# Turning cached attention keys on VectorE, sharing the runs of two sample groups, and 512-column matmuls for the memory keys and values

## The chip, the cores and the metric

The kernel runs on one core of a Trainium2 chip. The metric is the device time of one execution in microseconds, as the median over several executions. The trace is of one execution that the hardware profiler recorded.

## The reference

One inference step of a two-layer streaming encoder is computed for two groups of inputs at once: a prompt of 512 new frames, and 8 running streams (the samples) with 16 new frames each behind 256 cached ones. The part that matters here is the mixer of the first layer (forgetting attention, 16 heads of 64), and the keys and values of the memory for both layers:

```
def fox_mixer(h, q_pos, past, w_in, b_f, w_out):
    ...
    k_all = jnp.concatenate([past[0], k], axis=1)
    v_all = jnp.concatenate([past[1], v], axis=1)
    ...
    s = jnp.einsum('bqhd,bkhd->bhqk', qb, k_all).astype(jnp.float32) * FOX_SCALE
    s = s + jnp.moveaxis(cqb, 1, 2)[..., None] - ck
    p = masked_softmax(s, mask).astype(v_all.dtype)
    return jnp.einsum('bhqk,bkhd->bqhd', p, v_all)

def memory_kv(mem, g_mem, w_x_kv):
    m_l = rms_normalize(mem)[None] * g_mem[:, None, None, :]
    kv = jnp.einsum('lbnd,lde->lbne', m_l, w_x_kv)
    k, v = jnp.split(kv, 2, axis=-1)
```

For the samples `past[0]` is the cached keys, `cache_fox_k`, of shape (1, 8, 256, 16, 64). `mem_prompt` has 256 rows of 1024, and `w_x_kv` is (2, 1024, 2048). All is float32.

## The kernel before

The first phase, `fox_phase`, goes through the 16 heads in eight pairs. For each pair `pr` three lists of steps are merged by `merge`: `prompt_list` (attention of the prompt, 9 steps), `sample_list` (attention of the samples, 14 steps) and a fill of projections for the next pairs: `k_list`, `v_list`, `q_list` and `out_list`. A step stands at the place (i + 0.5) / length of its list, and the merged order is the order in which instructions are emitted. The tile framework's planner then makes each engine's queue out of that order by priority, modelled durations and free buffers; at run time each queue is in order. The pools name how many buffers a tile has (`bufs`); an instruction that needs a buffer waits until the last reader of its former content is done.

A big matrix product is made of three passes of float32r matmuls (`PASSES`: high by high, high by low, low by high). `load_w` brings a weight unit of 128 x 1024 values into `raw` (2 buffers), ScalarE casts it to `whi` (L150), and VectorE subtracts to get `wlo` (L151), with 3 buffers each. All of the kernel's DMAs are issued on SyncE's queue (SP).

`sample_list` handles the eight streams as two groups of four (`bq` = 0 and 1), one after the other. For each group `load` fetches the cached keys (`kr`, L654, one buffer, tokens on the partitions, 1,024 pieces of 512 bytes) and values (`vr`, L656), `keys` turns 8 blocks of 128 x 128 by TensorE in two visits of 4 (L664), and the results are copied out of PSUM into `KT` by VectorE (L668) for the first half and ScalarE (L670) for the second. `scores` does the matmuls of L685 and the softmax, and builds a block-diagonal copy of the new frames' weights on VectorE (L694). `trans` turns the weights (L701), `values` multiplies by the values (L710), and `turn` turns the result back (L717) and gates it (L722). VectorE also copies the new keys into `KT` (L658).

`mem_list` makes the memory's keys and values of one layer. Its first group of steps normalises the 256 memory rows and turns them into `mT`; eight more groups each handle 256 output columns: a load of two weight units, two products of 24 matmuls with 256 columns (one for each 128 memory rows, each in its own PSUM bank and in two parts), a copy to `mrow` by ScalarE (L373), and a store. Of the 18 groups of both layers, the first 7 are fill of pair 6, the next 9 of pair 7, and the last 2 come after all pairs.

## Time and profile before

| | |
|---|---|
| median of 3 runs | 2115.81 us (2113.45 to 2122.21) |
| the profiled execution: time | 2118.55 us |
| the profiled execution: span of the core | 2116.8 us |
| mean granted TensorE clock | 0.998 |
| TensorE matmul busy | 2066.9 us, 98% of the span |
| TensorE weight loads busy | 1857.4 us, 88% |
| VectorE, ScalarE, GpSimd busy | 1393.1, 900.0 and 176.0 us (66%, 43%, 8%) |

The span is the time from the first to the last instruction of the core; 1.75 us of the execution's time lie outside it. Busy times are unions of the instructions' spans. A matmul's span begins before the one ahead of it has ended, so one matmul's duration is longer than the step from one matmul to the next. In rows of the trace PE is TensorE's matmuls, PEld its weight loads, DVE VectorE, ACT ScalarE, POOL GpSimd, and SP SyncE with a q for its queue of DMA issues.

### The profile page before, as it was taken

The page shows a single profiled execution, that of the slowest core. Times are in us where ns is not written, and L with a number is a line of the kernel's source. Part 1 is how long each engine was busy: PE and PEld are TensorE (multiplying, and loading weights), DVE is VectorE, ACT ScalarE, POOL GpSimd, SP SyncE. Part 2 cuts the span into 40 slices and gives each one's busy share as a digit, 9 for nine tenths or more (in the row PEclk, how much of TensorE's full clock was granted, in tenths as well). Part 3 has the DMA queues.
Part 4 walks back from the last instruction along what each step waited for, and adds up shares of the span by engine and source line. Part 5 has one row for each costly group of instructions (what it writes and reads, how often), then busy time and mean ns, then how long its engine had stood idle before and what let it go on. Part 6 is the DMA issues. An engine that isn't in the chain of part 4 may idle for free. (4 is left out here: it accounts for less than half of the span.)

```text
span 2116.8 us, 35888 instructions
## 1 busy us (share of the span) xinstructions
PE 2066.9 (98%) x14189; PEld 1857.4 (88%) x14189; DVE 1393.1 (66%) x2695; ACT 900.0 (43%) x1793; POOL 176.0 (8%) x362
## 2 busy tenths in 40 slices
PE   7999999999999999999999999999999999999998
PEld 7988888889987899999998978887887799999997
DVE  4454555564646796686686567767546896686686
ACT  4444444454443453343344455554443453343342
POOL 1121212120100000000001301100100000000000
PEclk9999999999999999999999999999999999999999
DMA  7443434477555322232221331112554322232221
GB/s 225 130 137 107 139 112 130 147 230 224 166 165 172 100 72 83 85 91 79 81 80 50 92 95 39 53 44 77 164 167 157 100 74 84 83 92 79 80 81 60
DMA packets 279279, 234.33 MB, mean 111 GB/s; under 512 B 15668, under 2 KB 255924, under 8 KB 279112
## 3 DMA queue, kind: packets, MB, share of 16 engines
q1 hardware_dynamic: 279112, 232.05, 36.0%
q8 instruction: 112, 1.84, 0.4%
q14 instruction: 55, 0.45, 0.1%
HBM read 214.80 MB, written 17.21 MB: 110 GB/s over the span
## 5 line engine op out<-in xcount | busy, mean ns | idle before, releaser
L204 PE MATMUL mm<-hT,whi 128*128 128x320 f32 x1744 | 291.5, 313 | 3.8 <-ACT hT L222 3.8
L204 PEld LDWEIGHTS mm<-hT,whi 128*128 128x128 f32 x1744 | 260.9, 188 | 9.8 <-ACT hT L222 5.2
L151 DVE TENSOR_TENSOR wlo<-raw,whi 128x1024 fp32r<-128x1024 f32 (+4 forms) x145 | 170.1, 1176 | 144.2 <-ACT whi L150 84.8
L318 DVE TENSOR_TENSOR X<-mm,X 128x512 f32<-128x512 f32 x270 | 182.8, 686 | 123.1 <-PE mm L204 121.8
L150 ACT CAST whi<-raw 128x1024 fp32r<-128x1024 f32 (+4 forms) x145 | 144.6, 1002 | 150.8 <-PE mm L204 103.4
L204 PE MATMUL mm<-whi,oT 128*128 128x512 f32 x544 | 182.9, 410 | 1.9 <-DVE X L318 1.1
L1103 ACT CAST whi<-tw 128x512 fp32r<-128x512 f32 (+1 forms) x120 | 91.9, 765 | 213.7 <-PE mm L204 127.5
L204 PE MATMUL mm<-whi,aT 128*128 128x512 f32 x560 | 173.0, 390 | 0.3 <-ACT aT L1068 0.3
L204 PE MATMUL mm<-hT,wlo 128*128 128x320 f32 x872 | 156.8, 312 | 0.0
L204 PEld LDWEIGHTS mm<-hT,wlo 128*128 128x128 f32 x872 | 133.4, 188 | 3.2 <-issue 3.1
L204 PE MATMUL mm<-whi,hT 128*128 128x256 f32 (+2 forms) x800 | 127.5, 298 | 2.4 <-ACT whi L150 1.5
L204 PE MATMUL mm<-s,whi 128*128 128x320 f32 x768 | 128.2, 309 | 0.0
L204 PEld LDWEIGHTS mm<-whi,aT 128*128 128x128 f32 x560 | 104.4, 188 | 22.6 <-ACT aT L1068 1.2
L232 POOL TENSOR_SCALAR rstd<-ss 128x1 f32<-128x1 f32 x49 | 17.2, 352 | 1266.0 <-ACT hn L230 1261.5
L204 PEld LDWEIGHTS mm<-whi,oT 128*128 128x128 f32 x544 | 96.6, 189 | 23.2 <-issue 3.7
L204 PEld LDWEIGHTS mm<-whi,hT 128*128 128x128 f32 x800 | 110.0, 193 | 7.7 <-issue 3.9
L204 PEld LDWEIGHTS mm<-s,whi 128*128 128x128 f32 x768 | 116.6, 188 | 0.0
L1104 DVE TENSOR_TENSOR wlo<-tw,whi 128x512 fp32r<-128x512 f32 (+1 forms) x120 | 103.4, 862 | 18.9 <-ACT whi L1103 18.4
L204 PE MATMUL mm<-wlo,oT 128*128 128x512 f32 x272 | 109.1, 401 | 0.0
L204 PE MATMUL mm<-wlo,aT 128*128 128x512 f32 x280 | 108.8, 389 | 0.0
L1103 ACT CAST whi<-raw 128x1024 fp32r<-128x1024 f32 x44 | 46.3, 1052 | 131.7 <-PE mm L204 72.3
L204 PE MATMUL ps_s<-whi,aT 128*128 128x512 f32 x320 | 98.6, 389 | 0.0
(340 smaller groups left out, 4280.5 us busy)
## 6 DMA issues: line engine op xcount, KB each, us to landing
rawg<-w_ffn_gu SPq DMA_DIRECT2D x80, 512.0 KB
raw<-w_ffn_down SPq DMA_DIRECT2D x44, 512.0 KB
raw<-w_x_kv SPq DMA_DIRECT2D x32, 512.0 KB
kr<-cache_mem_k SPq DMA_DIRECT2D x64, 256.0 KB
vr<-cache_mem_v SPq DMA_DIRECT2D x32, 512.0 KB
raw<-w_fox_in SPq DMA_DIRECT2D x30, 512.0 KB
kr<-cache_fox_k SPq DMA_DIRECT2D x16, 512.0 KB
vr<-cache_fox_v SPq DMA_DIRECT2D x16, 512.0 KB
```

The costliest lines, as they stand in the source:

```text
L150: A.copy(hi[:, 0:m], raw[:, 0:m])
L151: V.tensor_tensor(lo[:, 0:m], raw[:, 0:m], hi[:, 0:m].bitcast(F32), ALU.subtract)
L204: T.matmul(st["ps"][:, 0:n], lhsT=l, rhs=r, start=(j == 0), stop=(j == m - 1))
L232: G.tensor_scalar(r, ss, EPS, None, ALU.add)
L318: V.tensor_tensor(xs, ps, xs, ALU.add)
L1103: A.copy(hi[:, o:o + m], src)
L1104: V.tensor_tensor(lo[:, o:o + m], src, hi[:, o:o + m].bitcast(F32), ALU.subtract)
```

## The change

Four things change in `fox_phase` and `mem_list`.

- The cached keys arrive in another order. Token 32m + j of a stream lies on partition j of a block of 32 partitions, and four DMAs for each group, one for each 32 channels of the pair's 128, fill the four blocks of partitions. `V.transpose` then turns blocks of 32 x 32 straight from `kr` into `KT`, 512 columns an instruction, two for each group. There are no TensorE transposes of keys, and no copies out of PSUM for them. `kr` has 2 buffers and `KT` 3.
- The copy of the new keys into `KT` and the block-diagonal product move from VectorE to GpSimd.
- The two groups of streams go through one list of 13 steps: both loads first, then four `keys` steps, two `bias` steps, one `scores` step with the matmuls of both groups in two PSUM banks, two `trans` steps, one `values` step into one bank, and one `turn` step with two transposes and two gating products twice as wide.
- `mem_list` has four groups for 512 output columns each in place of eight for 256. A group holds two PSUM banks open, one for each 128 memory rows, and goes through the 1024 input rows in four parts: a weight unit of 256 rows by 512 columns, then 6 matmuls of 512 columns into each bank. Each part's unit is loaded one part ahead. Of the 10 groups now, 4 are in pair 6, 5 in pair 7 and 1 after the pairs.

```diff
@@ -354,23 +354,36 @@
             to_T(h, d["mT"], t * P, KD)
 
         groups = [[gains, lambda: norm(0), lambda: norm(1)]]
-        for h in range(4):
+        for c0 in range(0, D, 512):
             for i in range(2):
-                c0 = i * D + h * XD
                 u = {}
 
-                def load(u=u, c0=c0):
-                    u["w"] = load_w([(0, XD, w_kv[:, c0:c0 + XD])])
-                    u["row"] = pool().tile([P, 2, XD], F32, tag="mrow", name="mrow", bufs=2)
-
-                def store(u=u, i=i, h=h):
-                    S.dma_start(outs[i][:, :, h * XD:(h + 1) * XD], u["row"])
-                    S.dma_start(kvd[l][i].rearrange("(t p) n -> p t n", p=P)[:, :, h * XD:(h + 1) * XD], u["row"])
-
-                L = [load]
-                for t in range(2):
-                    L += gemm(lambda u=u, t=t: as_ops(d["mT"], slice(t * P, (t + 1) * P), u["w"], slice(0, XD), KD),
-                              XD, lambda ps, u=u, t=t: A.copy(u["row"][:, t, :], ps[:, 0:XD]), parts=2)
+                def load(m, u=u, c=i * D + c0):
+
+                    if m == 0:
+                        u["row"] = pool().tile([P, 2, 512], F32, tag="mrow", name="mrow", bufs=2)
+                    u[m] = load_w([(0, 512, w_kv[:, c:c + 512])], k0=2 * m, kt=2, per=2)
+
+                def part(m, u=u):
+                    for t in range(2):
+                        if m == 0:
+                            u["ps", t] = psum_mm()
+                        ops = [(d["mT"][ai][:, 2 * m + k, t * P:(t + 1) * P], u[m].get(wi, k))
+                               for wi, ai in PASSES for k in range(2)]
+                        for n, (l, r) in enumerate(ops):
+                            T.matmul(u["ps", t], lhsT=l, rhs=r, start=(m == 0 and n == 0), stop=(m == 3 and n == 5))
+                        if m == 3:
+                            A.copy(u["row"][:, t, :], u["ps", t])
+
+                def store(u=u, i=i, c0=c0):
+                    S.dma_start(outs[i][:, :, c0:c0 + 512], u["row"])
+                    S.dma_start(kvd[l][i].rearrange("(t p) n -> p t n", p=P)[:, :, c0:c0 + 512], u["row"])
+
+                L = [lambda load=load: load(0)]
+                for m in range(4):
+                    if m < 3:
+                        L.append(lambda load=load, m=m: load(m + 1))
+                    L.append(lambda part=part, m=m: part(m))
                 groups.append(L + [store])
         return groups
 
@@ -378,7 +391,7 @@
     def fox_phase():
         w_in = I["w_fox_in"][0]
         w_out = I["w_fox_out"][0]
-        ck = I["cache_fox_k"][0].rearrange("b (tt t) h d -> t (b tt) (h d)", t=P)
+        ck = I["cache_fox_k"][0].rearrange("b (m j) h d -> j (b m) (h d)", j=32)
         cv = I["cache_fox_v"][0].rearrange("b (tt t) h d -> t (b tt) (h d)", t=P)
         ko = O["fox_k_p"][0, 0].rearrange("(t p) h d -> p t (h d)", p=P)
         vo = O["fox_v_p"][0, 0].rearrange("(t p) h d -> p t (h d)", p=P)
...
@@ -650,28 +663,23 @@
                 d = {}
 
                 def load(bq):
-                    d["kr"] = fp.tile([P, 8, P], F32, tag="kr", name="kr", bufs=1)
-                    S.dma_start(d["kr"], ck[:, 8 * bq:8 * bq + 8, pr * P:(pr + 1) * P])
-                    d["vr"] = fp.tile([P, 8, P], F32, tag="vr", name="vr", bufs=2)
-                    S.dma_start(d["vr"], cv[:, 8 * bq:8 * bq + 8, pr * P:(pr + 1) * P])
-                    d["KT"] = fp.tile([P, 4, KS], F32, tag="KT", name="KT", bufs=2)
-                    V.tensor_copy(d["KT"][:, :, PAST:KS],
+
+                    kr = d["kr", bq] = fp.tile([P, 32, 32], F32, tag="kr", name="kr", bufs=2)
+                    for i in range(4):
+                        c0 = pr * P + 32 * i
+                        S.dma_start(kr[32 * i:32 * i + 32], ck[:, 32 * bq:32 * bq + 32, c0:c0 + 32])
+                    d["vr", bq] = fp.tile([P, 8, P], F32, tag="vr", name="vr", bufs=2)
+                    S.dma_start(d["vr", bq], cv[:, 8 * bq:8 * bq + 8, pr * P:(pr + 1) * P])
+                    d["KT", bq] = fp.tile([P, 4, KS], F32, tag="KT", name="KT", bufs=3)
+                    G.tensor_copy(d["KT", bq][:, :, PAST:KS],
                                   ks[pr][1][:, bq * 64:(bq + 1) * 64].rearrange("p (b t) -> p b t", t=TS))
 
-                def keys(b2):
-                    pt = psum_t()
-                    for i in range(4):
-                        T.transpose(out=pt[:, i * P:(i + 1) * P], in_=d["kr"][:, 4 * b2 + i, :], identity=ident)
-                    src = pt[:, :].rearrange("p (b t) -> p b t", t=PAST)
-                    dst = d["KT"][:, 2 * b2:2 * b2 + 2, 0:PAST]
-                    if b2 == 0:
-                        V.tensor_copy(dst, src)
-                    else:
-                        A.copy(dst, src)
-
-                def scores(bq):
-                    Q = qs_[pr][1]
-                    pw = d["pw"] = pw_tile()
+                def keys(bq, b2):
+                    V.transpose(d["KT", bq][:, 2 * b2:2 * b2 + 2, 0:PAST],
+                                d["kr", bq][:, 16 * b2:16 * b2 + 16, :].rearrange("p (b m) i -> p b (m i)", b=2))
+
+                def bias(bq):
+                    pw = d["pw", bq] = pw_tile()
                     r0 = 16 * pr + 8 * bq
                     S.dma_start(pw[:, 0:KS], csd[r0:r0 + 8].unsqueeze(1).broadcast_to([8, TS, KS]))
                     jk = small.tile([P, TS], F32, tag="jk", name="jk")
@@ -680,53 +688,60 @@
                                            op0=ALU.mult, op1=ALU.add, accum_out=cqs)
                     G.tensor_scalar(pw[:, 0:KS], pw[:, 0:KS], -1.0, cqs, ALU.mult, ALU.add)
                     G.tensor_tensor(pw[:, PAST:KS], pw[:, PAST:KS], cm16, ALU.add)
-                    sp = psum_s()
-                    for b in range(4):
-                        T.matmul(sp[32 * b:32 * b + 32, 0:KS], lhsT=Q[:, 4 * bq + b, :], rhs=d["KT"][:, b, :],
-                                 start=True, stop=True, tile_position=(0, 32 * b))
-                    nm = small.tile([P, 1], F32, tag="nm", name="nm")
-                    V.tensor_tensor_reduce(out=pw[:, 0:KS], in0=sp[:, 0:KS], in1=pw[:, 0:KS], scale=-1.0,
-                                           scalar=3.0e38, op0=ALU.add, op1=ALU.min, accum_out=nm)
-                    ss = small.tile([P, 1], F32, tag="ssum", name="ssum")
-                    A.activation(pw[:, 0:KS], pw[:, 0:KS], AF.Exp, scale=-1.0, bias=nm, accum_out=ss)
-                    softmax_tail(pw, ss, KS)
-                    bm = cst[:, C_BM + P * bq:C_BM + P * (bq + 1)]
-                    V.tensor_tensor(pw[:, 272:400].rearrange("p (b t) -> p b t", t=TS),
-                                    pw[:, PAST:KS].unsqueeze(1).broadcast_to([P, B, TS]),
-                                    bm.rearrange("p (b t) -> p b t", t=TS), ALU.mult)
-
-                def trans():
+
+                def scores():
+
+                    Q = qs_[pr][1]
+                    sps = [psum_s() for _ in range(2)]
+                    for bq in range(2):
+                        for b in range(4):
+                            T.matmul(sps[bq][32 * b:32 * b + 32, 0:KS], lhsT=Q[:, 4 * bq + b, :],
+                                     rhs=d["KT", bq][:, b, :], start=True, stop=True, tile_position=(0, 32 * b))
+                    for bq in range(2):
+                        pw, sp = d["pw", bq], sps[bq]
+                        nm = small.tile([P, 1], F32, tag="nm", name="nm")
+                        V.tensor_tensor_reduce(out=pw[:, 0:KS], in0=sp[:, 0:KS], in1=pw[:, 0:KS], scale=-1.0,
+                                               scalar=3.0e38, op0=ALU.add, op1=ALU.min, accum_out=nm)
+                        ss = small.tile([P, 1], F32, tag="ssum", name="ssum")
+                        A.activation(pw[:, 0:KS], pw[:, 0:KS], AF.Exp, scale=-1.0, bias=nm, accum_out=ss)
+                        softmax_tail(pw, ss, KS)
+                        bm = cst[:, C_BM + P * bq:C_BM + P * (bq + 1)]
+                        G.tensor_tensor(pw[:, 272:400].rearrange("p (b t) -> p b t", t=TS),
+                                        pw[:, PAST:KS].unsqueeze(1).broadcast_to([P, B, TS]),
+                                        bm.rearrange("p (b t) -> p b t", t=TS), ALU.mult)
+
+                def trans(bq):
                     pt = psum_t()
                     for i, o in enumerate((0, P, 272)):
-                        T.transpose(out=pt[:, i * P:(i + 1) * P], in_=d["pw"][:, o:o + P], identity=ident)
-                    d["PT"] = pt_tile()
-                    A.copy(d["PT"][:, 0:3 * P], pt[:, 0:3 * P])
+                        T.transpose(out=pt[:, i * P:(i + 1) * P], in_=d["pw", bq][:, o:o + P], identity=ident)
+                    d["PT", bq] = pt_tile()
+                    A.copy(d["PT", bq][:, 0:3 * P], pt[:, 0:3 * P])
 
                 def values():
                     op = psum_o()
-                    for kt in range(3):
-                        for b in range(4):
-                            rhs = d["vr"][:, 2 * b + kt, :] if kt < 2 else vs[g][:, TT - 1, cs_]
-                            T.matmul(op[32 * b:32 * b + 32, 0:P], lhsT=d["PT"][:, kt * P + 32 * b:kt * P + 32 * b + 32],
-                                     rhs=rhs, start=(kt == 0), stop=(kt == 2), tile_position=(0, 32 * b))
-                    d["osb"] = fp.tile([P, P], F32, tag="osb", name="osb", bufs=1)
-                    A.copy(d["osb"], op[:, 0:P])
-
-                def turn(bq):
+                    for bq in range(2):
+                        for kt in range(3):
+                            for b in range(4):
+                                rhs = d["vr", bq][:, 2 * b + kt, :] if kt < 2 else vs[g][:, TT - 1, cs_]
+                                T.matmul(op[32 * b:32 * b + 32, bq * P:(bq + 1) * P],
+                                         lhsT=d["PT", bq][:, kt * P + 32 * b:kt * P + 32 * b + 32],
+                                         rhs=rhs, start=(kt == 0), stop=(kt == 2), tile_position=(0, 32 * b))
+                    d["osb"] = fp.tile([P, 2, P], F32, tag="osb", name="osb", bufs=1)
+                    A.copy(d["osb"], op[:, 0:2 * P].rearrange("p (q n) -> p q n", q=2))
+
+                def turn():
                     pt = psum_t()
-                    T.transpose(out=pt[:, 0:P], in_=d["osb"], identity=ident)
-                    s0 = NP + 64 * bq
+                    for bq in range(2):
+                        T.transpose(out=pt[:, bq * P:(bq + 1) * P], in_=d["osb"][:, bq], identity=ident)
                     for hh in range(2):
                         rs = slice(64 * hh, 64 * hh + 64)
-                        sv = sg[pr][rs, s0:s0 + 64].rearrange("p (b q) -> p b q", q=TS)
-                        V.tensor_tensor(sv, pt[rs, 0:P].rearrange("p (b h q) -> p b h q", h=2, q=TS)[:, :, hh, :],
+                        sv = sg[pr][rs, NP:NT].rearrange("p (b q) -> p b q", q=TS)
+                        V.tensor_tensor(sv, pt[rs, 0:2 * P].rearrange("p (b h q) -> p b h q", h=2, q=TS)[:, :, hh, :],
                                         sv, ALU.mult)
 
-                L = []
-                for bq in range(2):
-                    L += [lambda bq=bq: load(bq), lambda: keys(0), lambda: keys(1), lambda bq=bq: scores(bq),
-                          trans, values, lambda bq=bq: turn(bq)]
-                return L
+                return [lambda: load(0), lambda: load(1)] + \
+                    [lambda bq=bq, b2=b2: keys(bq, b2) for bq in range(2) for b2 in range(2)] + \
+                    [lambda: bias(0), lambda: bias(1), scores, lambda: trans(0), lambda: trans(1), values, turn]
 
             def finish(pr):
                 if pr < 7:
@@ -774,12 +789,12 @@
                 if pr % 2 == 0 and pr < 6:
                     fill += v_list(pr // 2 + 1)
                 if pr == 6:
-                    fill += sum(mems[:7], [])
+                    fill += sum(mems[:4], [])
                 if pr == 7:
-                    fill += sum(mems[7:16], [])
+                    fill += sum(mems[4:9], [])
                 merge(prompt_list(pr), sample_list(pr), fill)
                 finish(pr)
-            for f in sum(mems[16:], []):
+            for f in sum(mems[9:], []):
                 f()
             w = load_w([(0, 1024, w_out)], k0=6, kt=2, per=1)
```

Not shown is one hunk, in which the tile `osb` of the decay sums is made twice as wide because it shares its buffer.

## Rows read from the trace of the kernel before

**Rows 1.** The page's first part: busy time, share of span, instructions.

```profile
PE 2066.9 (98%) x14189; PEld 1857.4 (88%) x14189; DVE 1393.1 (66%) x2695; ACT 900.0 (43%) x1793; POOL 176.0 (8%) x362
```

**Rows 2.** Stretches: six pairs, then pairs with memory; last columns clock, DMA share, GB/s.

```profile
97.00:400.00 303.00, 302.52 (x2493) 264.58 (x2492) 167.94 (x463) 128.84 (x295) 60.09 (x123) 1.00 0.42 120
400.00:525.00 125.00, 119.42 (x1061) 111.27 (x1059) 66.16 (x129) 61.80 (x118) 19.21 (x30) 1.00 0.71 224
```

**Rows 3.** Waits of TensorE matmuls, 0 to 560 us: total, times, longest.

```profile
PE ps_t L246 <- DVE hn L277: 8.7, 1, 8.7
...
PE ps_t L701 <- DVE pw L331: 1.7, 2, 1.5
```

**Rows 4.** Timeline of TensorE, 164 to 176 us: start, duration, what, count.

```profile
167.43 1.34 PE L204 MATMUL mm<-hT,wlo 128*128 128x320 f32 x8
168.60 0.60 PE L664 MATMUL ps_t<-cst,kr 128*128 128x128 f32 x4
168.96 2.59 PE L204 MATMUL mm<-hT,whi 128*128 128x320 f32 x16
171.48 0.96 PE L600 MATMUL ps_s<-kT,qT 64*128 64x512 f32 x6
```

**Rows 5.** Timeline of TensorE, 518 to 530 us.

```profile
517.76 1.12 PE L204 MATMUL mm<-whi,mT 128*128 128x256 f32 x8
...
519.21 1.12 PE L204 MATMUL mm<-whi,mT 128*128 128x256 f32 x8
...
526.06 0.39 PE L204 MATMUL mm<-wlo,oT 128*128 128x512 f32 x1
526.29 0.39 PE L204 MATMUL mm<-whi,oT 128*128 128x512 f32 x1
```

**Rows 6.** Groups of TensorE, 0 to 700 us: count, busy us, mean ns.

```profile
L204 PE MATMUL mm<-hT,whi 128*128 128x320 f32 x768 | 129.6, 315 | 1.9 <-ACT hT L222 1.9
...
L664 PE MATMUL ps_t<-cst,kr 128*128 128x128 f32 x128 | 19.7, 273 | 0.0
```

**Rows 7.** Groups of VectorE, 0 to 700 us.

```profile
L151 DVE TENSOR_TENSOR wlo<-raw,whi 128x1024 fp32r<-128x1024 f32 x85 | 105.3, 1239 | 104.6 <-ACT whi L150 61.3 <-PE mm L204 39.6 <-PE ps_s L600 2.0
...
L668 DVE COPY KT<-ps_t 128x512 f32<-128x512 f32 x16 | 10.9, 684 | 10.0 <-PE ps_t L664 10.0
...
L331 DVE TENSOR_SCALAR pw<-pw,rc 128x512 f32<-128x512 f32 x16 | 7.6, 484 | 0.4
...
L694 DVE TENSOR_TENSOR pw<-pw,cst 128x128 f32<-128x128 f32 x16 | 4.6, 289 | 0.4
```

**Rows 8.** Groups of ScalarE, 0 to 700 us.

```profile
L670 ACT COPY KT<-ps_t 128x512 f32<-128x512 f32 x16 | 9.3, 581 | 5.6 <-PE ps_t L664 5.6
```

**Rows 9.** Groups of GpSimd, 0 to 700 us.

```profile
L592 POOL TENSOR_SCALAR_AFFINE_SELECT pw<-pw 128x128 f32<-128x128 f32 x64 | 20.1, 326 | 2.1
...
L738 POOL TENSOR_TENSOR oT<-sig,oT 128x640 fp32r<-128x640 f32 x8 | 13.6, 1696 | 74.9 <-ACT oT L737 74.9
```

**Rows 10.** DMA from 42 to 46 us: packets and sizes, then share of 16 engines.

```profile
DMA packets 2914, 0.30 MB, mean 75 GB/s; under 512 B 2689, under 2 KB 2913, under 8 KB 2913
...
q1 hardware_dynamic: 2913, 0.28, 60.8%
```

**Rows 11.** The same from 700 to 1000 us.

```profile
DMA packets 37908, 25.26 MB, mean 84 GB/s; under 512 B 752, under 2 KB 34176, under 8 KB 37888
...
q1 hardware_dynamic: 37888, 24.98, 28.2%
```

**Rows 12.** Timeline of SP's queue, 100 to 240 us.

```profile
147.31 0.38 SPq L654 DMA_DIRECT2D kr<-cache_fox_k  x1
...
160.26 0.37 SPq L656 DMA_DIRECT2D vr<-cache_fox_v  x1
```

**Rows 13.** Waits of all engines, 400 to 525 us: total, times, longest.

```profile
ACT whi L150 <- DMA raw<-w_x_kv: 21.3, 13, 4.9
```

More of the change, by code (lines that the diff above doesn't have):

```diff
@@ L451, in past @@
                             cl = nl
-                        ct = fp.tile([P, P], F32, tag="osb", name="osb", bufs=1)
+                        ct = fp.tile([P, 2 * P], F32, tag="osb", name="osb", bufs=1)[:, 0:P]
                         V.tensor_copy(ct[0:r].rearrange("p (c b h) -> p c b h", b=B, h=2),
```

## The prediction

> **What bounds the kernel now.** I read the page's busy times first, then stretches of the phase that changes, then what TensorE waits for there, then single instructions. TensorE's matmuls cover 98% of the span, its weight loads 88%; VectorE has 66%, ScalarE 43%, GpSimd 8% [rows 1]. The stretches say it more sharply: between 97 and 400 us, six head pairs, TensorE is busy for 302.52 of 303 us at granted clock 1.00, which is the upper level of 2.4 GHz, while VectorE is at 55% and the DMA engines at 42%. From 400 to 525 us, where the memory work fills, TensorE has 119.42 of 125 us and the DMA share is 0.71 [rows 2]. Waits are few: the largest, 8.7 us, is once at the start, and what a sample's weight transposes wait for softmax is 1.7 us in all [rows 3]. So the time is the sum of the steps from one matmul to the next, and work taken from TensorE should come off almost whole, unless something else then makes it wait. A duration is not a step, though: four key transposes in a row take 0.60 us, not four times 273 ns [rows 4, 6].
>
> **Key transposes off TensorE.** There are 128, in 32 visits of 4 [rows 6]. Inside a visit the step is (0.60 - 0.27) / 3 = 0.11 us, so four steps are 0.44. The second reading is from outside: from 167.43 to 171.48 us, 4.05 us, lie 24 matmuls of 320 columns and one visit. With a step of (2.59 - 1.34) / 8 = 0.156 for those (two runs that differ by 8) the visit costs 0.30; with (1.34 - 0.315) / 7 = 0.146, one run less the duration of its last, it costs 0.54 [rows 4, 6]. I take 0.44: 32 x 0.44 = 14.1 us saved, between 9.6 and 17.1.
>
> The Trainium skill, page "TensorE: Matmul & The Clock Gate", section "Part 4: PE-mode transpose", gives about 275 ns for a 128 x 128 transpose within a kernel. The trace agrees for the duration (273 ns) but not for the step; by the page's figure, as an estimate, 128 of them would be 35 us and the whole sum 41 us rather than 20.
>
> **The same transposes on VectorE.** 32 instructions of 128 x 512, a form that the trace does not show. Nearest are the PSUM copy of that size, 684 ns, and a scaling from SBUF to SBUF, 484 ns; above I bound it by twice the copy, 1.37 us [rows 7]. I take 0.69, since a transpose, like that copy, reads one source and writes one: 22.1 us. Off go 16 copies (10.9 us) and 16 products (4.6 us) [rows 7], the small copies of new keys, and half of the gating products, so VectorE gains at most 6.6 us of work, or 28 at the upper end, over 430 us in which it is 55% busy [rows 2]: no bound either way. ScalarE loses 16 copies, 9.3 us [rows 8]. Both cost nothing while TensorE sets the pace. What hides the new transposes is their lead: `kr` has two buffers, and its successor can be fetched as soon as a group is turned, well over half a pair (some 25 us) before use; before, a fetch at 147.31 served transposes at 168.60, 21 us on [rows 4, 12]. Were that cover gone, VectorE's queue would stand, with the subtractions that make `wlo` (1.24 us each [rows 7]) and the evictions behind it, and TensorE after them.
>
> **GpSimd** gets 16 copies and 16 products of 128 columns. Between 0.33 us (a 128 x 128 select) and 128/640 of 1.70 us, also 0.34, I take 0.35 each [rows 9]: 11 us on an engine at 20% [rows 2]. Only the product lies in a chain: scores, softmax, product, `trans`. It was 0.29 us on VectorE [rows 7] and now adds a handover between engines; that is at most a few tenths of a microsecond for each pair, where the wait has so far been 1.7 us in all [rows 3].
>
> **Shared runs.** Scores, values and turn become one visit for each pair instead of two: 24 visits less. What entering and leaving a visit costs I can only bound, by the two readings above: 0 to 0.24 us, so 0 to 5.8 us. Against it, two softmaxes now stand between one `scores` and the first `trans`, and both score banks are held at once, so the prompt's next scores may wait. I take -3 and +2, net -1 us.
>
> **Memory in 512 columns.** 768 matmuls become 384 twice as wide. Twelve of 256 columns take 519.21 - 517.76 = 1.45 us, 0.121 each; one of 512 takes 526.29 - 526.06 = 0.23 us [rows 5]. So 92.9 us becomes 88.3: -4.6. Casts, subtractions and bytes of weights stay, 32 units of 512 KB. TensorE is idle for 5.6 of the 125 us here [rows 2]. A unit's buffers now come free after its own part rather than at the end of a group, and loads are a part ahead; I credit a third, -1.9. The bounds are 0 (the stage is then paced by weights) and -10.2.
>
> **DMA.** The keys come in 64 DMAs of 1,024 pieces of 128 bytes where 16 of 1,024 pieces of 512 bytes were: 65,536 pieces for 16,384. No row has such pieces alone. Lower bound: from 42 to 46 us, with 2,689 of 2,914 packets under 512 bytes, 60.8% of 16 engines for 4 us is 38.9 us, or 13.4 ns a packet. Upper bound: from 700 to 1000 us, a mean of 660 bytes, 28.2% of 4,800 us over 37,888 packets is 35.7 ns [rows 10, 11]. Before, by size, about 28 ns x 16,384 / 16 = 29 us. Now 55 to 146 us, spread over 430: the share rises from 0.42 to 0.48 or 0.69 in the pairs, from 0.71 to 0.77 or 0.98 with the memory. A group's keys occupy all engines for 3.4 to 9.1 us instead of 1.8, and whatever SP has issued behind them comes that much later. I take the lower end, since the packets there are nearest in size, and +2 us for weights that come late: ScalarE already waits 21.3 us for the memory's weights [rows 13]. SP's own order loosens for keys, but `vr` (2 buffers) must now wait for the shared `values` step of the pair before; it used to wait as well, to 160.26 [rows 12], and is needed a pair later.
>
> The Trainium skill, "DMA: Bandwidth & Descriptors", section "Specifications", asks for at least 512 bytes for line rate and says that smaller writes become read-modify-writes, which speaks against this change. The trace agrees that small packets carry less for their time (0.28 MB in 38.9 us of engine time is 7.2 GB/s an engine, against 18.5 GB/s in the later stretch) and shows no price beyond that [rows 10, 11].
>
> **The sum.** -14.1 - 4.6 - 1.9 - 1 + 2 = -19.6 us. From the profiled execution's 2118.55 that is 2099; that execution lay 2.7 us above the median of 2115.81, so for the median I say 2096. A change of 0.5%, 10.6 us, is about what a measurement here can tell from none.
>
> **The rivals.**
> - *More comes free.* The transposes at 17.1, shared visits at 5.8, all the idle time of the memory stage, no late weights: -17.1 - 5.8 - 4.6 - 5.6 = -33.1, so 2083. For it: VectorE, ScalarE and two PSUM banks are relieved at once. Against: every term would have to come out at its best.
> - *A transpose really occupies TensorE for its 273 ns.* 128 x 0.273 = 35 us, sum -41, 2075. Against it stand the four in 0.60 us. This is the TensorE page's figure taken as a price.
> - *The gain turns into waits.* Transposes and narrower matmuls go, but the memory stage is paced by weights (0 of its 6.5), and the first `trans` and the prompt's scores wait 1 us more in each of 8 pairs: -14.1 + 8 = -6, 2110. For it: weights are waited for already [rows 13]. That the change does nothing at all, because matmul busy time is a modelled figure, falls in here.
> - *Slower: key fetches block the queue.* At 9.1 us for each group, the engines carry 0.98 of what they can in the memory stage, and a weight unit issued behind a fetch lands up to 7.3 us late. If 4.5 of those 7.3 are not covered, 8 pairs lose 36 us in place of the 2 above, and the sum is -21.6 + 36 = +14, so 2130. It decides from about 6 us for a fetch, or 24 ns a packet, halfway between the bounds. The DMA page's rule would act this way.
>
> **How the numbers follow.** Forecast (2089 to 2107 of its own) 0.53, of which 0.05 falls within 0.5%; more comes free 0.14; a transpose at its duration 0.02; waits 0.21, all within 0.5%; slower 0.10, of which 0.02 is within. That makes faster 0.64, same 0.28, slower 0.08. The range leaves about half of the best case and the slow one outside: 2085 to 2115.
>
> **What would show it.** No TensorE instruction reads `kr`; VectorE has 32 transposes near 0.69 us; matmuls of 512 columns on `mT` at steps of 0.23 us; packets of 128 bytes near 13 ns, and the DMA share near 0.48 in the pairs; waits of TensorE on GpSimd's product in tenths. I am wrong if VectorE's transposes wait for `kr` by DMA, if waits on `raw` grow well past 21 us, or if the transposes take over 1 us.

## The result, and the profile after

The changed kernel takes 2102.75 us (median of 4 runs, 2100.78 to 2105.32), the kernel before beside it 2115.89 us. The ratio is 0.9929 [0.9913, 0.9945]. By the medians 13.1 us came off, by the ratio 15.0. The forecast was 19.6 off and a time of 2096 within 2085 to 2115: the side is right, the time lies in the range, a quarter to a third of the expected gain is missing. The profiled execution after took 2105.32 us, with a span of 2103.5.

The page after, its busy times and its line of packets, against [rows 1]:

```profile
PE 2051.7 (98%) x13677; PEld 1824.2 (87%) x13677; DVE 1394.5 (66%) x2663; ACT 889.7 (42%) x1753; POOL 193.8 (9%) x394
...
DMA packets 316650, 234.26 MB, mean 111 GB/s; under 512 B 81716, under 2 KB 281012, under 8 KB 316488
```

TensorE has 512 matmuls fewer: 128 transposes of keys and 384 of the memory's 768. Its share of the span is still 98%, so it still sets the pace, and VectorE's sum did not move (1393.1 to 1394.5 us).

The stretches after, with the columns of [rows 2]:

```profile
97.00:400.00 303.00, 299.44 (x2412) 257.60 (x2412) 175.10 (x442) 126.14 (x281) 77.26 (x153) 1.00 0.55 134
400.00:525.00 125.00, 118.56 (x694) 92.52 (x691) 69.03 (x122) 61.80 (x104) 20.61 (x35) 0.99 0.72 234
```

Here is the first sign of what is missing. In the six pairs TensorE was idle for 0.48 of 303 us before; now it is idle for 3.56. The granted clock is 1.00 there as before, so in this stretch the steps did not get slower by the clock; from 400 to 525 us it is 0.99 where it was 1.00, and more on it stands under "Where the loss shows". The DMA share went from 0.42 to 0.55 in the pairs, and hardly moved with the memory (0.71 to 0.72).

The new operations, each against its price in the prediction. VectorE's groups, 0 to 700 us:

```profile
L678 DVE STREAM_TRANSPOSE KT<-kr 128x512 f32<-128x512 f32 x32 | 21.5, 691 | 0.0
```

GpSimd's groups, 0 to 700 us:

```profile
L605 POOL TENSOR_SCALAR_AFFINE_SELECT pw<-pw 128x128 f32<-128x128 f32 x64 | 22.3, 366 | 1.2
L753 POOL TENSOR_TENSOR oT<-sig,oT 128x640 fp32r<-128x640 f32 x8 | 16.1, 2018 | 86.5 <-ACT oT L752 86.5
L709 POOL TENSOR_TENSOR pw<-pw,cst 128x128 f32<-128x128 f32 x16 | 10.1, 634 | 26.6 <-DVE pw L331 24.3 <-DVE rc L330 2.3
```

TensorE's timeline at the last of the memory's matmuls:

```profile
507.69 1.07 PE L374 MATMUL mm<-whi,mT 128*128 128x512 f32 x4
508.60 0.62 PE L374 MATMUL mm<-wlo,mT 128*128 128x512 f32 x2
509.05 1.07 PE L374 MATMUL mm<-whi,mT 128*128 128x512 f32 x4
509.96 0.62 PE L374 MATMUL mm<-wlo,mT 128*128 128x512 f32 x2
510.42 0.64 PE L204 MATMUL mm<-whi,oT 128*128 128x512 f32 x2
```

The transpose on VectorE takes 0.691 us (0.69 was taken), and its idle column is 0.0: it never waits for `kr`. Six matmuls of 512 columns take 509.05 - 507.69 = 1.36 us, a step of 0.227 (0.23 was taken). GpSimd's product takes 0.634 us, nearly twice the 0.35 assumed (0.461 to 0.467 in three of the kernels below), and GpSimd's other work became slower too (326 to 366 ns, 1696 to 2018 ns, [rows 9]).

The last line, 510.42 us, serves below as a milestone: the first matmul of the output projection that follows the memory's last one. Up to there every kernel has done the same work, and all that the change touches: 9,999 or 10,000 matmuls are left in each of the fourteen traces. Behind it the code is the same; yet the rest of the span, from milestone to end, is between 1588.4 and 1595.2 us in these traces, so a span alone is uncertain by some microseconds, and the milestone says better where the time came from. It is a reading of one execution too, and not exact: it lies between 508.66 and 512.07 us in the whole change and three kernels that hardly differ from it (the table below). The kernel before passes it at 523.52:

```profile
523.04 0.64 PE L204 MATMUL mm<-wlo,mT 128*128 128x256 f32 x4
523.52 0.62 PE L204 MATMUL mm<-whi,oT 128*128 128x512 f32 x2
```

So 13.1 us were gained by the milestone, of 13.3 by which the two spans differ. The waits of TensorE, 40 to 530 us, show what is new there beside [rows 3]:

```profile
PE mm L374 <- ACT mT L222: 2.3, 1, 2.3
PE mm L204 <- DVE X L318: 2.0, 3, 1.1
PE ps_t L636 <- DVE pw L331: 1.8, 1, 1.8
PE mm L374 <- ACT mrow L376: 1.6, 1, 1.6
PE ps_t L636 <- ACT PT L718: 1.5, 3, 0.7
PE ps_t L716 <- DVE pw L331: 0.9, 2, 0.4
```

None of these is large and none is the product on GpSimd. They are waits for the memory's turned rows (`mT`, once, 0.3 us before), softmaxes (`pw`), evictions (`X`) and copies (`PT`, `mrow`) that come a little late, spread over the phase.

### The profile page after: what moved, and what is told of

It is laid out like the page before. It is cut to its first block, busy times and chain, and to the rows that moved or that the text cites. A ratio compares the mean times of both kernels' runs of the same rounds, so it can differ in the third digit from the quotient of the medians.

```text
span 2103.5 us, 34831 instructions
## 1 busy us (share of the span) xinstructions
PE 2051.7 (98%) x13677; PEld 1824.2 (87%) x13677; DVE 1394.5 (66%) x2663; ACT 889.7 (42%) x1753; POOL 193.8 (9%) x394
## 5 line engine op out<-in xcount | busy, mean ns | idle before, releaser
L232 POOL TENSOR_SCALAR rstd<-ss 128x1 f32<-128x1 f32 x49 | 16.3, 332 | 1266.1 <-ACT hn L230 1261.7
L1119 DVE TENSOR_TENSOR wlo<-tw,whi 128x512 fp32r<-128x512 f32 (+1 forms) x120 | 103.4, 862 | 18.9 <-ACT whi L1118 18.2
```

Of the source, the lines that this page charges most:

```text
L232: G.tensor_scalar(r, ss, EPS, None, ALU.add)
L1119: V.tensor_tensor(lo[:, o:o + m], src, hi[:, o:o + m].bitcast(F32), ALU.subtract)
```

## The experiments

Two questions were open: which part gives the gain, and where the rest of the forecast went. The first four kernels take the parts one by one. Ratios are to the kernel before, measured beside each.

**Keys alone.** `keys_only` has VectorE's transposes, the new fetch and the buffers of `kr` and `KT`, and nothing else; the groups stay one after the other, and copy and product stay on VectorE.

```diff
-                    pt = psum_t()
-                    for i in range(4):
-                        T.transpose(out=pt[:, i * P:(i + 1) * P], in_=d["kr"][:, 4 * b2 + i, :], identity=ident)
...
+                    V.transpose(d["KT"][:, 2 * b2:2 * b2 + 2, 0:PAST],
+                                d["kr"][:, 16 * b2:16 * b2 + 16, :].rearrange("p (b m) i -> p b (m i)", b=2))
```

> The kernel before with the cached keys alone turned by VectorE (keys in 128-byte pieces, two kr buffers, three KT buffers); groups of streams one after the other, block-diagonal product and new-key copy on VectorE, memory in 256 columns. Theory A (each term is as predicted, the shared runs lose what is missing): TensorE loses 32 visits of 0.44 us, so -14 us, near 2102. Rival B (VectorE's transposes come in bursts that hold up the evictions of the projections, and give half back): -7 us, near 2109. Rival C (the memory stage gives nothing): says -14 here too.

Measured: 2101.93 us, ratio 0.9928 [0.9914, 0.9941], 15.2 us less. TensorE's timeline at the milestone:

```profile
508.90 0.64 PE L204 MATMUL mm<-wlo,mT 128*128 128x256 f32 x4
509.38 0.62 PE L204 MATMUL mm<-whi,oT 128*128 128x512 f32 x2
```

523.52 - 509.38 = 14.1 us by the milestone, the sum of the prediction (32 visits of 0.44). That it agrees to a tenth is luck: `keys_twice`, below, does the same work on TensorE and passes the milestone at 507.34, 16.2 us ahead. The keys alone give as much as the whole change.

**Memory alone.** `mem_only` takes the hunk of `mem_list` and the new counts of groups, and nothing else:

```diff
-        for h in range(4):
+        for c0 in range(0, D, 512):
...
-                    fill += sum(mems[:7], [])
+                    fill += sum(mems[:4], [])
```

> The kernel before with the memory part alone changed (512 columns, two open banks, units of 256 rows by 512 columns). Theory A: -6.5 us, near 2109. Rival B: -6.5 too. Rival C (the stage is paced by weight units or by the softmax chains of the last two pairs, so that TensorE only idles longer): 0 to -2 us, near 2115, with TensorE's busy time in that stage down by about 5 us and its idle time up by as much.

Measured: 2114.21 us, ratio 0.9987 [0.9978, 0.9996]: about 2.8 us less, under half of the 6.5. Its trace shows no gain by the milestone: it passes there at 525.24, 1.7 us after the kernel before. TensorE's matmuls are busy for 505.2 us up to the milestone (506.3 before) and idle for 20.1 (17.2), and the granted clock is 0.86 from 25 to 50 us (0.93 before) and 0.99 from 400 to 525 (1.00 before). That TensorE idles longer is as rival C has it; its busy time falls by less than the 5 us that the rival named, and a part of the loss, from 25 to 50 us, lies ahead of the memory's matmuls.

**Shared runs alone.** `shared_only` takes the one list of 13 steps for both groups, with keys still turned by TensorE, and copy and product still on VectorE:

```diff
+                return [lambda: load(0), lambda: load(1)] + \
+                    [lambda bq=bq, b2=b2: keys(bq, b2) for bq in range(2) for b2 in range(2)] + \
+                    [lambda: bias(0), lambda: bias(1), scores, lambda: trans(0), lambda: trans(1), values, turn]
```

> The kernel before with the shared runs alone: one list of 13 steps for both groups of streams, but keys in 512-byte pieces turned by TensorE and copied out as before (two kr buffers, three KT buffers), block-diagonal product and new-key copy on VectorE, memory in 256 columns. Theory A: the two softmaxes one behind the other and the two held score banks make TensorE wait, +6 us, near 2122. Rival B and rival C: 24 visits fewer, -1 us or a little better, 2112 to 2115.

Measured: 2119.95 us, ratio 1.0005 [0.9995, 1.0016]: no gain, and a loss of at most 3.4 us, not to be told from none. Its milestone, 521.68, is 1.8 us ahead of the kernel before.

**Small pieces alone.** `pieces_only` is the kernel before, but each group's keys come in four DMAs of 128-byte pieces.

```diff
-                    S.dma_start(d["kr"], ck[:, 8 * bq:8 * bq + 8, pr * P:(pr + 1) * P])
+                    for i in range(4):
+                        c0 = pr * P + 32 * i
+                        S.dma_start(d["kr"][:, :, 32 * i:32 * i + 32], ck[:, 8 * bq:8 * bq + 8, c0:c0 + 32])
```

> The kernel before, but each group's keys fetched by four DMAs of 32 channels each, in 128-byte pieces, into the same places as before; all else as it was. It measures what the small pieces cost by themselves. Theory A and rival C: nothing that can be measured, 0 to +2 us, with a packet of 128 bytes near 16 ns and the DMA share in the six pairs near 0.5. A rival D (late weights behind the key fetches are what is missing): +5 us or more, and waits of ScalarE on raw by DMA longer.

Measured: 2118.64 us, ratio 1.0008 [0.9999, 1.0017]: no loss that could be told from none, at most 3.6 us. Its milestone, 525.86, is 2.3 us later, within what near copies differ by. The DMA queue between 97 and 400 us (packets, MB, share of 16 engines) in `pieces_only`:

```profile
q1 hardware_dynamic: 88312, 35.59, 50.2%
```

and in the kernel before:

```profile
q1 hardware_dynamic: 51566, 35.98, 41.2%
```

About the same bytes take 9.0% of 16 x 303 us more, 436 us of engine time. Six pairs turn 12,288 pieces into 49,152; with the 28 ns of the prediction for one of 512 bytes, that is (436 + 344) / 49,152 = 15.9 ns for a piece of 128, an estimate much nearer to the lower bound (13.4) than to the upper (35.7). And the weights are not later for it: ScalarE's wait for the memory's weights in `pieces_only` from 400 to 525 us is as in [rows 13]:

```profile
ACT whi L150 <- DMA raw<-w_x_kv: 21.2, 15, 4.9
```

The small pieces by themselves thus do not make the weights late. Nor does that wait go with the time: it is 28.3 us in `keys_mem`, the fastest kernel below, and 23.7 after the whole change. Two explanations were left: that parts do not add (keys and memory together give no more than one of them), or that the shared runs, neutral by themselves, cost something once the keys are off TensorE. The next four kernels set these against each other.

**Keys and memory together.** `keys_mem` is `keys_only` with the hunk of `mem_list`; it lacks the shared runs and GpSimd's new work:

```diff
                 L = []
                 for bq in range(2):
                     L += [lambda bq=bq: load(bq), lambda: keys(0), lambda: keys(1), lambda bq=bq: scores(bq),
                           trans, values, lambda bq=bq: turn(bq)]
                 return L
```

> Keys turned by VectorE and the memory part in 512 columns, but the groups of streams one after the other as before, with the block-diagonal product and the new-key copy on VectorE: the whole change without its shared runs and without the move to GpSimd. Measured so far: keys alone -15 us, memory alone -3, shared runs alone 0, the whole change -15. Theory A, as it now stands (the two gains add, and the shared runs together with VectorE's transposes give about 3 us back): -18 us, near 2099, ratio 0.9915. Rival B (the memory part's gain does not add, because the weight units then wait behind the key fetches): -15, ratio 0.993, no better than keys alone.

Measured: 2096.38 us, ratio 0.9905 [0.9893, 0.9918], 20 us less. This beats both kernels. The whole change stands at 0.9929 [0.9913, 0.9945], so the middles are 0.0024 apart, 5 us, and the intervals overlap by 0.0005. Three near copies of the whole change, below, lie at 0.9925 to 0.9932, so the distance is not one measurement's chance. TensorE's timeline at the milestone:

```profile
506.18 0.62 PE L374 MATMUL mm<-wlo,mT 128*128 128x512 f32 x2
506.64 0.64 PE L204 MATMUL mm<-whi,oT 128*128 128x512 f32 x2
```

It passes the milestone 16.9 us ahead of the kernel before and 3.8 ahead of the whole change. The parts add (by themselves -15.2 and -2.8); what the whole change has besides costs.

**The product back on VectorE.** `after_vprod` is the whole change with one letter different:

```diff
-                        G.tensor_tensor(pw[:, 272:400].rearrange("p (b t) -> p b t", t=TS),
+                        V.tensor_tensor(pw[:, 272:400].rearrange("p (b t) -> p b t", t=TS),
```

> The whole change with the block-diagonal product on VectorE as before, not on GpSimd (0.29 us there against a measured 0.63 us on GpSimd, in the chain from scores to the weight transposes). Theory A: the chain gets shorter, but VectorE, already in a burst there, gets 0.6 us a pair more: within 1 us of the whole change, 0.993. Rival B (the slower product on GpSimd is what is missing): 3 us or more faster than the whole change, 0.9915 or less.

Measured: 2102.49 us, ratio 0.9932 [0.9921, 0.9944]: no difference from the whole change. The 0.634 us on GpSimd is not the cost. The copy of the new keys stayed on GpSimd here; `shared_scores`, below, has it on VectorE and loses all the same.

**Each VectorE transpose twice.** `keys_twice` is `keys_only` with a loop of two around `V.transpose`; the second writes the same values again.

```diff
+                    for _ in range(2):
+                        V.transpose(d["KT"][:, 2 * b2:2 * b2 + 2, 0:PAST],
```

> Keys alone on VectorE, as in the run of keys alone, but each transpose done twice over the same place: 32 more transposes of 0.69 us, 22 us more on VectorE, no other change. Theory A (VectorE's time is covered): within 3 us of keys alone, 2100 to 2105. Rival B (VectorE's bursts cost about half of what they take): +11 us against keys alone, near 2113.

Measured: 2100.89 us, ratio 0.9926 [0.9913, 0.9939], as `keys_only`. VectorE's groups, 0 to 700 us, in `keys_twice`:

```profile
L665 DVE STREAM_TRANSPOSE KT<-kr 128x512 f32<-128x512 f32 x64 | 43.2, 694 | 0.9 <-DMA kr<-cache_fox_k 0.6
```

There are 64 of them at 694 ns, so 21 us more on VectorE, and the time stands still. The cover that the prediction named is there with room to spare. The milestone comes at 507.34, 2.0 us ahead of `keys_only`, with no more than TensorE's same work: the granted clock of this trace is 1.00 from 400 to 525 us, that of `keys_only` 0.99.

**Scores for each group by itself.** `split_scores` is the whole change with scores, softmax and `trans` done group after group again; both loads still come first, and `values` and `turn` stay shared.

```diff
+                L = [lambda: load(0), lambda: load(1)]
+                for bq in range(2):
+                    L += [lambda bq=bq, b2=b2: keys(bq, b2) for b2 in range(2)]
+                    L += [lambda bq=bq: bias(bq), lambda bq=bq: scores(bq), lambda bq=bq: trans(bq)]
+                return L + [values, turn]
```

> The whole change, except that the scores, their softmax and the weight transposes stay a step for each group, with keys, bias, scores and trans of group 0 ahead of those of group 1; only the loads, the values and the turn are shared. Theory A (what is lost are the two softmaxes in one burst on VectorE, which hold up the evictions of the output projection): -3 us against the whole change, ratio 0.9915 to before, and fewer waits of TensorE on the eviction of X. Rival B (what is lost comes from the shared values and turn, or from later releases of vr): no change against the whole, 0.993.

Measured: 2113.96 us, ratio 0.9978 [0.9967, 0.9989]. It became worse, by some 10 us against the whole change: a clear miss. Undoing the shared scores in this way does not bring the gain back. The list of steps is another one too, though, and with it the places at which the steps fall between those of the prompt and the fill. So place became a theory of its own.

**The same steps at other places.** Two empty steps at the end of the list (`after_early`) move all others forward in the merged order, two behind the loads (`after_late`) move all but the loads back:

```diff
-                    [lambda: bias(0), lambda: bias(1), scores, lambda: trans(0), lambda: trans(1), values, turn]
+                    [lambda: bias(0), lambda: bias(1), scores, lambda: trans(0), lambda: trans(1), values, turn,
+                     lambda: None, lambda: None]
```

```diff
-                return [lambda: load(0), lambda: load(1)] + \
+                return [lambda: load(0), lambda: load(1), lambda: None, lambda: None] + \
```

> The whole change with two empty steps at the end of the samples' list of 13, so that each of its steps stands earlier against the prompt's: the shared scores at 8.5/15 = 0.57, midway between the prompt's scores at 0.39 and 0.72, instead of at 0.65. No instruction is added or left out. Theory A (the shared scores hold both score banks and put two softmaxes in VectorE's queue just ahead of the prompt's last scores): with more room behind them 3 to 6 us come back, 2097 to 2100, ratio 0.990 to 0.9915. Rival B (the loss lies in the shared values and turn, or in vr released late): no change, 0.993.

> The whole change with two empty steps behind the two loads, so that the shared scores stand at 10.5/15 = 0.70, right ahead of the prompt's last scores at 0.72; the loads move from 0.04 and 0.12 to 0.03 and 0.10. No instruction is added or left out. Theory A: slower than the whole change by 3 us or more, ratio 0.9945 or more, with more waits of TensorE for the score banks. Rival B: no change, 0.993.

Measured: 2101.15 us, 0.9925 [0.9912, 0.9939], and 2101.13 us, 0.9931 [0.9919, 0.9944]. Neither differs from the whole change. Moving the whole list by a step or two is not it.

**One shared step at a time, on the best version.** `shared_values` is `keys_mem` with `values` and `turn` shared; `shared_scores` is `keys_mem` with `scores` alone shared. Their lists:

```diff
+                    L += [lambda bq=bq: load(bq), lambda bq=bq: keys(bq, 0), lambda bq=bq: keys(bq, 1),
+                          lambda bq=bq: soft(bq), lambda bq=bq: trans(bq)]
+                return L + [values, turn]
```

```diff
+                    L += [lambda bq=bq: load(bq), lambda bq=bq: keys(bq, 0), lambda bq=bq: keys(bq, 1)]
+                L.append(soft)
+                for bq in range(2):
+                    L += [lambda bq=bq: trans(bq), lambda bq=bq: values(bq), lambda bq=bq: turn(bq)]
```

> Keys on VectorE and memory in 512 columns as in the run of both together, with the groups of streams one after the other up to the weight transposes, and then one shared values step and one shared turn step for both. Block-diagonal product and new-key copy on VectorE. That the place of the shared scores in the list makes no difference has put the bursts at that place out as the cause. Theory A2 (the shared scores as such, 16 matmuls that need the last of both groups' keys and hold both banks, cost the 5 us): no loss here, ratio 0.9905. Rival B (the shared values and turn, with cached values and weights of both groups held until the end of the pair, cost it): 0.9925 or more.

> The other half: one shared scores step for both groups' keys, then transposes of weights, values and turn a step for each group as before; keys on VectorE, memory in 512 columns, product and new-key copy on VectorE. Theory A2: the whole loss is here, 0.9925 to 0.993. Rival B: no loss here, 0.9905.

Measured: 2098.84 us, 0.9911 [0.9895, 0.9927], and 2107.40 us, 0.9951 [0.9933, 0.9969]. Shared values cost little or nothing (0.0006, 1.3 us, within the intervals); shared scores cost 0.0046, some 10 us, more than was expected of them.

**Where the loss shows.** TensorE's busy time in the 490 us from 40 to 530 shows a part of it, with the columns of [rows 2]. In `keys_mem`:

```profile
40.00:530.00 490.00, 482.26 (x3580) 407.51 (x3579) 284.80 (x686) 218.23 (x451) 97.23 (x188) 1.00 0.60 160
```

after the whole change:

```profile
40.00:530.00 490.00, 477.40 (x3543) 404.94 (x3542) 274.51 (x634) 216.07 (x440) 111.29 (x218) 0.99 0.60 160
```

and in `split_scores`:

```profile
40.00:530.00 490.00, 473.27 (x3494) 396.13 (x3494) 263.36 (x621) 210.63 (x428) 105.61 (x211) 1.00 0.60 158
```

| | idle, 40 to 530 us | idle, 0 to milestone | milestone | ratio |
|---|---|---|---|---|
| before | 7.6 | 17.2 | 523.52 | 1 |
| `keys_only` | 10.0 | 16.3 | 509.38 | 0.9928 |
| `keys_twice` | 9.1 | 15.9 | 507.34 | 0.9926 |
| `shared_values` | 6.1 | 14.3 | 507.34 | 0.9911 |
| `keys_mem` | 7.7 | 16.8 | 506.64 | 0.9905 |
| `after_early` | 13.3 | 21.9 | 510.80 | 0.9925 |
| whole change | 12.6 | 20.3 | 510.42 | 0.9929 |
| `after_late` | 10.0 | 18.9 | 508.66 | 0.9931 |
| `after_vprod` | 11.6 | 20.3 | 512.07 | 0.9932 |
| `shared_scores` | 11.5 | 20.1 | 512.43 | 0.9951 |
| `split_scores` | 16.7 | 22.4 | 517.05 | 0.9978 |

Idle is the stretch less the busy time. A stretch with fixed ends holds more of the work behind the milestone the faster a kernel is, so the second column is the better one: 14.3 to 17.2 us in the kernels that keep their gain, 18.9 to 22.4 in the six that lose some. Within each set idle time does not order them, and it is not all: the whole change is 3.8 us behind `keys_mem` at the milestone with 3.5 us more of it, `split_scores` 10.4 with 5.6 more. The other 4.8 us of `split_scores` lie in busy time and have no cause shown here.

A second part is the clock. From 40 to 97 us, which is mostly the first pair, the rows are, in `keys_mem` and after the whole change:

```profile
40.00:97.00 57.00, 56.67 (x456) 52.03 (x455) 26.76 (x72) 24.65 (x54) 9.86 (x22) 1.00 0.72 166
40.00:97.00 57.00, 55.20 (x420) 51.45 (x420) 25.38 (x65) 23.41 (x50) 10.91 (x26) 0.97 0.66 146
```

Of the wait of 1.8 us for the prompt's softmax (L636 on L331, above), all lies between 74 and 78 us, and behind it, from 78 to 82 us, the granted clock is 0.62: for a part of that stretch TensorE is at the lower of its two levels, 1.2 GHz. In `keys_mem` TensorE is never idle there and the clock is 1.00. `shared_scores` has the same wait (1.9 us) and 0.61, `after_early` and `after_late` 2.2 and 1.95 us and 0.58 and 0.63; `after_vprod` has the wait too (2.05 us) and 1.00 behind it. What a lower clock costs can be read from the 64 runs of the kernel before that were taken beside the experiments: those granted 0.999 took 2115.9 us on average, 0.998 2117.8, 0.997 2118.9 and 0.996 2121.9, about 1.8 us for each 0.001. The 19 runs of the whole change and its three near copies were granted 0.9968 on average and took 2101.9, the four of `keys_mem` 0.9982 and 2096.9. By this estimate some 2.5 of these 5 us are clock, which no run here tells apart from the waits that come before it.

At the end of the memory work in `split_scores` TensorE even waits 2.07 us for a cast of weights; its timeline:

```profile
514.06 1.42 PE L374 MATMUL mm<-whi,mT 128*128 128x512 f32 x5 [2.07 <-ACT whi L150]
515.32 0.73 PE L374 MATMUL mm<-wlo,mT 128*128 128x512 f32 x2
...
517.05 0.64 PE L204 MATMUL mm<-whi,oT 128*128 128x512 f32 x2
```

Two more things can be read in the trace of the whole change. First, the shared visit is not one visit. TensorE's timeline, 178 to 195 us:

```profile
180.87 0.73 PE L204 MATMUL mm<-whi,oT 128*128 128x512 f32 x2 [1.12 <-DVE X L318]
...
181.77 0.65 PE L698 MATMUL ps_s<-KT,Qbd 128*32 128x272 f32 x2
182.34 0.55 PE L636 MATMUL ps_t<-cst,pw 128*128 128x128 f32 x3
...
189.08 1.12 PE L698 MATMUL ps_s<-KT,Qbd 128*32 128x272 f32 x14
...
194.00 0.91 PE L716 MATMUL ps_t<-cst,pw 128*128 128x128 f32 x3 [0.43 <-DVE pw L331]
```

The planner puts 2 of the matmuls of L698 at 181.77 and the other 14 at 189.08, with prompt work between: here it saved no visit, and the scores that were begun at 181.77 were not complete before 189. In all five pairs between 109 and 360 us the 16 are split so, as 2 + 14 or 10 + 6. Second, the score matmuls cover more time. Their busy time from 109 to 360 us (TensorE, then weight loads) in `keys_mem`:

```profile
109.00:360.00 251.00, 6.66 (x80) 1.57 (x80) 1.00 0.60 140
```

and after the whole change:

```profile
109.00:360.00 251.00, 8.82 (x80) 2.67 (x80) 1.00 0.60 141
```

The same 80 matmuls cover 2.2 us more, though none became longer (392 to 417 ns in both): two visits of 8 cover 0.67 us each, a pair split into 2 and 14 covers 0.65 + 1.12. In `shared_only`, where two of the five pairs kept their 16 together, such a run covers 1.12, less than two visits. In `split_scores` they are back at 6.66, so this comes with the split run, while the idle time of `split_scores` comes without it. The spans overlap those of their neighbours, so how much of the 2.2 us is lost is not shown.

## Why the prediction was right, and which step failed

- **What bounds the kernel** was read rightly: TensorE sets the pace, and work taken from it came off the time. 21 us more on VectorE changed nothing (`keys_twice`).
- **Key transposes off TensorE**: right in mechanism and size. Forecast -14.1; -14.1 by the milestone and -15.2 by the median of `keys_only`, -16.2 by the milestone of `keys_twice`. The price by steps held, within some 2 us. That a transpose occupies TensorE for its 273 ns (rival, 35 us for 128) is refuted. The figure of the Trainium skill, "TensorE: Matmul & The Clock Gate", section "Part 4: PE-mode transpose", about 275 ns for one, agrees with the duration in [rows 6] but is no price in a stream of matmuls: the runs show 14.1 / 128 = 0.11 us each, 0.13 by the 16.2 of `keys_twice`.
- **VectorE's transposes**: 0.691 us for 0.69; they cost nothing, and waited 0.0 us for `kr`.
- **GpSimd**: the copy took less than taken, 0.237 us, the product nearly twice as much, and that cost nothing that shows (`after_vprod`).
- **Memory in 512 columns**: the matmuls' step was right (0.227 for 0.23), the sum too large: -2.8 us by itself, -4.9 by ratios on top of the keys (0.9928 to 0.9905), -2.7 by the milestone, where -6.5 stood. Of the third of the idle time that was credited half came at the most: 5.6 us before, 4.7 in `keys_mem`, 6.4 after and in `mem_only`. ScalarE's wait for the memory's weights is no shorter; from 400 to 525 us after:

```profile
ACT whi L150 <- DMA raw<-w_x_kv: 23.7, 16, 5.4
```

- **DMA**: the choice of the lower bound was right (15.9 ns a piece), and the +2 for late weights is at most 3.6 and not to be told from 0. The share in the pairs rose further than the 0.48 of the lower bound, to 0.51 with the pieces alone and 0.55 after, where the same stretch also holds more bytes (40.11 MB for 35.98). The Trainium skill, "DMA: Bandwidth & Descriptors", section "Specifications", asks for 512 bytes and more for line rate; the engine time agrees (a 128-byte piece takes more than half as long as one of 512), but the kernel's time does not show it.
- **Shared runs, the step that failed**: "I take -3 and +2, net -1 us" was of the wrong sign. The whole change loses 5 us against the kernel without them and without the move to GpSimd (0.9929 to 0.9905), and shared scores alone lose 10 with nothing moved to GpSimd. The visits counted as saved are not all saved: the score run is split in all five pairs looked at, and its matmuls cover 2.2 us more. TensorE's idle time up to the milestone rises by 3.5 us, waits that were put at +2. The clock, which the sum left as it was, falls behind one of these waits, and is some 2.5 of the 5 us by the estimate above.

The sum as measured: -15.2 for the keys, -4.9 for the memory, +5.1 for the shared runs and what comes with them, -15.0 by ratios (0.9929 of 2115.9). The last two terms are differences of measured ratios, so that this closes is no check of it. The median difference is 13.1, so the terms are known to some 2 us. Of the rivals, the gain that turns into waits came nearest in kind: not through the memory stage and the prompt's scores as told, but by the order of the samples' steps. Its 2110 was too dark: it let the memory give nothing, and it put 8 us on waits where idle time rose by 3 up to the milestone.

What stays open is why the order costs as much as it does. `split_scores` and `shared_values` do nearly the same instructions (scores and `trans` for each group, `values` and `turn` shared) and differ in that both loads come first, the bias is a step of its own and two small operations are on GpSimd; they stand 0.0067 apart, 14 us. The product on GpSimd and shifts of the whole list by two steps were tried and are not it, and small pieces are in `keys_mem` and `shared_values` too. `shared_scores` also puts the keys of both groups ahead of every score, so it does not tell sharing from order either. Which of the planner's choices makes the difference was not isolated, nor how much of it the clock would give back if the waits went. Nor is it shown why sharing costs nothing while TensorE still turns the keys (`shared_only`).

## What to carry to other kernels

When one engine sets the pace, price work taken from it by the step between its instructions, measured between its neighbours, and not by their durations; that number held to within some 2 us here. Merging two short independent chains into one is a saving only if the merged run stays together in the queue: look in the timeline for whether it does, and try the parts without the merge, as here the better kernel was the change without its merge and its move to GpSimd. Count a wait of the engine that sets the pace for more than its length: here a wait of 1.8 us had a stretch of lower clock behind it in most traces that have it, and the clock granted in a whole run went with its time. In a queue that a planner writes, a change of step order is a change of its own and needs a run of its own.

## What the runs showed of the hardware that was not expected

- VectorE's transpose of 32 x 32 blocks runs from SBUF to SBUF at 0.691 us for 128 x 512 float32, the time of a PSUM copy of that size (0.684 in [rows 7]), and not of the faster SBUF scaling (0.484).
- Four times as many DMA pieces of a quarter of the size raised the engines' share by 9 points and cost no time that could be measured (1.0008 [0.9999, 1.0017]).
- GpSimd's 128 x 128 select takes 310 to 326 ns in the kernels whose groups of streams go one after the other (`keys_mem` and `keys_twice` among them) and 347 to 400 ns in all that share a run, `shared_only` too, which gives GpSimd no new product. So it is neither VectorE's transposes nor the new products that slow it; what does was not tried.
